# A block product with seven terms for the first values of the second mixer, its weight sums loaded from HBM

## The chip, the cores and the metric

The kernel runs on one core of one Trainium2 chip. The metric is the device time of one execution in microseconds; lower is better. The kernel before takes 923.96 us, the median of three runs (923.92 to 923.99). Line numbers (L354) are those of the kernel before.

## The reference, cut to what matters

A trunk of two layers works on 256 tokens of width 1024. Each layer adds half of a SwiGLU network of width 2816, then a mixer, then half of a second such network. The mixer of the second layer, in which the change lies, is block-sparse attention; at 256 tokens there is one block, so it is causal softmax attention with 16 heads of 64:

```python
def c_mixer(x, w_in, w_out):
    q, k, v = jnp.split(x @ w_in, 3, axis=-1)          # x: (256, 1024), w_in: (1024, 3072)
    o = moba_attention(to_heads(q, 16, 64), to_heads(k, 16, 64), to_heads(v, 16, 64))
    return from_heads(o) @ w_out

for layer in range(2):
    h = h + 0.5 * swiglu(rms_norm(h, ffn1_norm[layer]), ...)
    h = h + mixer(rms_norm(h, mix_norm[layer]))         # layer 0: ab_mixer, layer 1: c_mixer
    h = h + 0.5 * swiglu(rms_norm(h, ffn2_norm[layer]), ...)
```

All is float32. What the change touches is `v = x @ w_in[:, 2048:2560]`, the values of the first eight heads: a product of 256x1024 by 1024x512.

## The kernel before, in words

**Numbers in two parts.** Every float32 operand of a matrix product is split into a high part (rounded to the matmul's format) and a low remainder. A product of two such operands is three matmuls: high by high, high by low, low by high (`mm3`, L353 to L356). ScalarE (ACT) writes the high part of a weight chunk (`whi`, L231), VectorE (DVE) the remainder (`wlo`, L238).

**The weight stream.** The host lays all weights out as chunks of up to 1 MB in the order of use (`weight_chunks`). `Stream` loads them on the SyncE queue into three raw buffers (`load_one`, L183), splits them into four pairs of high and low buffers (`SPL = 4`), and hands them to TensorE with `take()`; `free()` gives a pair back. So the split of a chunk can start when TensorE has finished the chunk four places before it, and a raw load when the split three places before it is done. `hold()` stops splits; `release(tc, behind, one)` lets one or all go, placed on ACT and DVE behind the instructions `behind`. `issue_after` orders instructions on one engine only. Within such bounds the order of each engine's instructions is made when the program is built, by a planner with its own estimates of durations; each engine then runs its list in order.

**Six stages** (phases 0 to 5): network, first mixer, network, network, second mixer (phase 4), network. In a network, 22 steps n (one per 1 MB chunk of gate or up weights) are followed by four column blocks c of the down projection, three chunks each. `Next.pair` (L396) adds a finished column block to the residual `x` and forms `xTh` and `xTl`, the scaled input of the next stage, 128 features by 256 tokens each.

**Sums that are made ahead.** The last network (phase 5) already forms most of its down projection by a block product with seven terms (Winograd's form of Strassen's scheme). The sums of weight blocks for it are made during phases 2 and 3: `begin_sums` loads a chunk (`blocks`, L631), makes sums on DVE (L635 to L641) and stores them in HBM (L647), from where the stream loads them later. `AHEAD` lists the steps at which this happens: (phase, n) with n = 4, 8, 12, 16 in phases 2 and 3, and (3, 19).

**The second mixer** (`c_mixer`, L1249) takes its chunks in this order: q0, k0 (queries and keys of heads 0 to 3), two value chunks of 512 features by 512 columns, q1, k1, q2, k2, two more value chunks, q3, k3, output projection. `first_tiles` (L1117) computes q0 and k0 and, between them, the norm of the input (`sums`, a power on GpSimd called `rstd`, `spread`). `token_block` (L1152) computes the values: for each of two chunks, each of two groups of 128 tokens and each of four feature tiles, three matmuls with 128 tokens stationary and 512 weight columns moving, into one PSUM bank for each token group. `put_v` then scales them into `vth` and `vtl` (L1169, L1170). There are eight PSUM banks. `scores`, `turn` (transposes, L1059) and `weighted` of the heads are hung between the tiles by `Slots`: `step()` counts, and the list says what is done at which count. In `put_k` GpSimd (POOL) copies and subtracts parts of the keys (L1000, L1002); in `scores` it scales the probabilities (L1050).

Of the kernel before, what the change touches and what calls it, by code (L numbers as in the profile page):

```python
# [10 lines left out]
F32 = mybir.dt.float32  # L11
# [40 lines left out]
def weight_chunks():  # L52
# [5 lines left out]

    def cols(m, c0, w, cuts=(), reset=0):
        n = CH // w  # L60
        for k in range(0, KD, n):
            add(m, k * 128, n, c0, c0 + w, SHIFT if w == 256 else 0, cuts, reset)

# [64 lines left out]
class Stream:  # L128
# [12 lines left out]
    def add(self, nk, w, shift, cuts, reset, summed, kind):  # L141

        cuts = (*(cuts or (() if reset else (nk / 2,))), nk)
        j = self.chunks
        self.chunks += 1
        for step in (1, 2) if kind != "N" else (0,):
            if step < 2 or kind == "X":
# [15 lines left out]
    def load_one(self, between=lambda i: None, first=False):  # L163
        u = self.loaded
        j, nk, w, loads, step = self.loads[u]
        i = (u - self.wide) % (RAW + SPARE) - RAW if self.wide is not None and u >= self.wide else -1
        raw = self.raw_pool.tile([128, CH], F32, name="raw") if i < 0 else self.spare[i]
        n = nk * w // loads
        for m in range(loads):
            between(m)  # L170
            cs = slice(m * n, (m + 1) * n)
            src = self.weights[j, m * 128 * n : (m + 1) * 128 * n].rearrange("(p c) -> p c", p=128)
            pieces = [(cs, self.sums[j][0] if step else src)]
            if step == 2:
# [25 lines left out]
    def split_parts(self):  # L200
# [20 lines left out]
        def split(a, r):  # L221
# [15 lines left out]
            else:  # L237
                self.made[u] = done, nc.vector.tensor_sub(lo, r, hi.bitcast(F32))  # L238

        if step:  # L240
            q = w // 2
# [70 lines left out]
def trunk(ctx: ExitStack, tc: tile.TileContext, a, out):  # L312
# [61 lines left out]
    class Next:  # L374
# [21 lines left out]
        def pair(self, i, p, row=None, pool=None, squares=True):  # L396
# [14 lines left out]
            return high, self.low  # L411

        def squares(self, i):

# [66 lines left out]

    nxt = None

# [139 lines left out]
    def begin_sums(fp, n):  # L623
# [27 lines left out]
        return sums  # L651

    def ffn(phase):
        nonlocal nxt
        with tc.tile_pool(name="fp", bufs=1) as fp:
            hT = [fp.tile([128, FT, S], F32R, name=n) for n in ("hTh", "hTl")]
# [22 lines left out]

            ready, ahead = [], []  # L680

# [23 lines left out]
            for n in range(FT):  # L705
# [13 lines left out]
                if (phase, n) in AHEAD:  # L719
                    ahead.append(begin_sums(fp, AHEAD.index((phase, n))))  # L720
                if (phase, n - 1) in AHEAD:
                    ahead.append(ahead.pop()())
                if (phase, n - 2) in AHEAD:
                    ahead.pop()()
                if n == late - 1:
# [17 lines left out]
            if last:  # L743
# [4 lines left out]
                return  # L748
            row = norm["half"]
            nxt = Next(phase + 1)  # L750
            for c in range(4):
                b = bank()
                for k0, n in DOWN:
# [7 lines left out]
                    if k0 + n == FT:  # L761
                        nxt.pair(c, b, row, fp)
                    st.free()

# [179 lines left out]

    def make_attention(mp, mask_cols, nheads, v, mix, rows=False):

# [107 lines left out]
        def turn(h):  # L1054
# [5 lines left out]
            if j == 0:  # L1060
                pts[p] = [mp.tile([128, 2, 384], F32R, name=n, bufs=2) for n in ("pth", "ptl")]
            return split(pts[p][0][:, j, :], pts[p][1][:, j, :], tp[:, :384])
# [53 lines left out]

    def first_tiles(put_q, put_k, step, places=None):  # L1117

# [8 lines left out]
        if not places:  # L1127
            st.free()
        w = st.take()
        tile_of(ps4[3], w, 1, range(4))  # L1130
# [5 lines left out]
        else:  # L1136
            nxt.sums()
        tile_of(ps4[2], w, 0)
        step()
        tile_of(ps4[3], w, 1, range(4, KD))  # L1140
# [5 lines left out]
        for j in range(2):  # L1146
            put_q(j, ps4[j])
            put_k(j, ps4[2 + j])
# [3 lines left out]
    def token_block(evict, step):  # L1152
# [9 lines left out]
        for t in range(NT):  # L1162
            evict(t, pb[t])

    def put_v(v, t, p, c0=0):
# [4 lines left out]
        nc.vector.scalar_tensor_tensor(v[1][:, t, cs], p, y, v[0][:, t, cs].bitcast(F32),  # L1170
                                       op0=ALU.mult, op1=ALU.subtract)

# [76 lines left out]
    def c_mixer(phase):  # L1249
        with tc.tile_pool(name="mp", bufs=1) as mp:  # L1250
            mix = mix_tiles(mp)
            v = v_tiles(mp, D)
            put_q, put_k, scores, turn, weighted, put_ks = make_attention(mp, slice(384, 768), 16, v, mix, True)
# [15 lines left out]
            for c in range(4):  # L1269
                if c:  # L1270
                    tiles(put_q, c, step)
                    tiles(put_k, c, step)
                else:
                    first_tiles(put_q, put_k, step)
                if c % 2 == 0:
                    token_block(lambda t, p: put_v(v, t, p, c * 256), step)
            project(mix, MIX2, phase, step)
            assert not slots.events


# [25 lines left out]
def _layout(a):  # L1306
# [6 lines left out]
    for j, (ms, layer, r, n, c0, c1, *how) in enumerate(chunks):  # L1313
# [3 lines left out]
        w = tiles(w)  # L1317
        if how[-1] != "N":
            w = w.reshape(128, 4, -1)[:, [3, 1, 0, 2]]
# [37 lines left out]
```

## Time and profile before

| what | value |
|---|---|
| median of 3 runs | 923.96 us |
| the profiled execution, its own time | 924.17 us |
| its span, first to last instruction | 922.4 us |
| granted TensorE clock | 0.999 |
| busy share of the span: TensorE matmuls, DVE, ACT, POOL | 99%, 75%, 57%, 9% |
| bytes moved by DMA | 202.15 MB, mean 219 GB/s |
| second mixer, value chunks on TensorE | 646.03 to 657.79 us |

The profiled execution lies 0.21 us over the median. A matmul's duration in the trace is modelled and overlaps its neighbours; what a matmul costs is the distance from its start to the start of the next. SyncE's and POOL's DMA queues share 16 DMA engines; a window's "DMA" is their mean busy share.

### The profile page before, as it was taken

To read this page: it belongs to the slowest core of one execution; us is meant where nothing else is said; L and a number is where in the kernel's file an instruction comes from. 1 tells how busy PE (TensorE), PEld (TensorE's weight loads), DVE (VectorE), ACT (ScalarE), POOL (GpSimd) and SP (SyncE) were. 2 spreads that over 40 slices of the span, in tenths; PEclk is the share of its full clock that TensorE was granted. 3 is DMA by queue.
4 is the path that set the end of the run, shared out by engine and by line. 5 is a ranking of instruction groups with operands and counts; after the bars stand their busy time and mean duration, and the time that the engine had idled before them with its cause. 6 is when DMAs were issued, how large, how long until landed. Compare 5 with 4: busy or idle time off the path is not lost.

```text
span 922.4 us, 18258 instructions
## 1 busy us (share of the span) xinstructions
PE 915.0 (99%) x7583; PEld 896.5 (97%) x7583; DVE 689.8 (75%) x1058; ACT 528.4 (57%) x808; POOL 80.8 (9%) x117
## 2 busy tenths in 40 slices
PE   9999999999999999999999999999999999999997
PEld 9999999999999999999999999999999999999886
DVE  7976556587888867655677666667778799978897
ACT  7754444468667545444564444455776777555574
POOL 0000000033310000000000000001565100000002
PEclk9999999999999999999999999999999999999999
DMA  9765554665256677766556878865533466855681
GB/s 325 272 228 183 180 195 174 228 226 181 93 183 230 220 281 266 296 238 218 187 209 236 305 272 313 318 216 192 184 137 137 119 230 225 277 191 206 223 310 60
DMA packets 33985, 202.15 MB, mean 219 GB/s; under 512 B 3904, under 2 KB 6208, under 8 KB 12528
## 3 DMA queue, kind: packets, MB, share of 16 engines
q1 hardware_dynamic: 32400, 197.79, 59.8%
q0 software_dynamic: 496, 1.77, 0.9%
q10 hardware_dynamic: 1008, 1.44, 0.5%
q8 instruction: 59, 0.97, 0.4%
q14 instruction: 22, 0.18, 0.1%
HBM read 188.14 MB, written 12.85 MB: 218 GB/s over the span
## 4 chain that ended last, share of the span: by engine, by line
PE 93%; issue 4%; DMA 2%; POOL 0%; DVE 0%; ACT 0%; POOLq 0%; DVEq 0%
PE bank L354 30%; PE bank L355 30%; PE bank L356 30%; DMA raw<-in_weights 1%; PE bank L1059 1%; DMA x<-blocks 1%; PE bank L601 1%; DMA xTl<-away 0%; POOL xTl L803 0%; DVE wlo L238 0%; PE bank L604 0%; PE bank L1021 0%; PE bank L1023 0%; PE bank L1022 0%; PE bank L1208 0%
## 5 line engine op out<-in xcount | busy, mean ns | idle before, releaser
L231 ACT ACTIVATE whi<-raw 128x1024 fp32r<-128x1024 f32 (+5 forms) x349 | 331.6, 994 | 280.4 <-issue 154.6
L238 DVE TENSOR_TENSOR wlo<-raw,whi 128x1024 fp32r<-128x1024 f32 (+5 forms) x349 | 390.6, 1149 | 78.8 <-ACT whi L231 77.8
L354 PE MATMUL bank<-xTh,whi 128*128 128x256 f32 x1600 | 442.7, 277 | 0.0
L356 PE MATMUL bank<-xTh,wlo 128*128 128x256 f32 x1600 | 441.8, 276 | 0.0
L355 PE MATMUL bank<-xTl,whi 128*128 128x256 f32 x1600 | 441.8, 276 | 0.0
L355 PEld LDWEIGHTS bank<-xTl,whi 128*128 128x128 f32 x1600 | 300.4, 188 | 0.0
L354 PEld LDWEIGHTS bank<-xTh,whi 128*128 128x128 f32 x1600 | 300.4, 188 | 0.0
L356 PEld LDWEIGHTS bank<-xTh,wlo 128*128 128x128 f32 x1600 | 300.4, 188 | 0.0
L356 PE MATMUL bank<-hTh,wlo 128*128 128x256 f32 x528 | 145.7, 276 | 0.0
L354 PE MATMUL bank<-hTh,whi 128*128 128x256 f32 x528 | 145.7, 276 | 0.0
L355 PE MATMUL bank<-hTl,whi 128*128 128x256 f32 x528 | 145.7, 276 | 0.0
L355 PEld LDWEIGHTS bank<-hTl,whi 128*128 128x128 f32 x528 | 99.1, 188 | 0.0
L354 PEld LDWEIGHTS bank<-hTh,whi 128*128 128x128 f32 x528 | 99.1, 188 | 0.0
L356 PEld LDWEIGHTS bank<-hTh,wlo 128*128 128x128 f32 x528 | 99.1, 188 | 0.0
L687 DVE TENSOR_TENSOR hm<-gs,bank 128x512 f32<-128x512 f32 x44 | 29.9, 683 | 45.4 <-PE bank L356 44.4
L954 POOL MEMSET k<- 64x256 f32 x12 | 3.2, 307 | 565.2 <-ACT whi L231 378.9
L684 DVE TENSOR_TENSOR gs<-bank,row 128x512 f32<-128x512 f32 x44 | 30.1, 686 | 21.3 <-PE bank L356 21.1
L354 PE MATMUL bank<-mixh,whi 128*128 128x256 f32 x128 | 35.7, 279 | 0.0
L356 PE MATMUL bank<-mixh,wlo 128*128 128x256 f32 x128 | 35.4, 277 | 0.0
L355 PE MATMUL bank<-mixl,whi 128*128 128x256 f32 x128 | 35.4, 276 | 0.0
L1050 POOL TENSOR_SCALAR pr<-pr,rl 128x128 f32<-128x128 f32 (+1 forms) x36 | 31.9, 899 | 29.5 <-DVE rl L1046 20.5
L359 ACT ACTIVATE hTh<-hm 128x512 fp32r<-128x512 f32 x44 | 27.1, 619 | 8.8 <-DVE hm L687 8.0
(231 smaller groups left out, 994.1 us busy)
## 6 DMA issues: line engine op xcount, KB each, us to landing
raw<-in_weights SPq DMA_DIRECT2D x139, 1024.0 KB, 5.0
raw<-in_weights SPq DMA_DIRECT2D x12, 768.0 KB, 4.8
blocks<-in_weights SPq DMA_DIRECT2D x9, 1024.0 KB, 10.0
blocks<-blocks SPq DMA_DIRECT2D x9, 1024.0 KB, 8.7
raw<-blocks SPq DMA_DIRECT2D x7, 1024.0 KB, 4.8
raw<-in_weights SPq DMA_DIRECT2D x6, 512.0 KB, 6.6
raw<-in_weights SPq DMA_DIRECT2D x7, 256.0 KB, 5.7
blocks<-block SPq DMA_DIRECT2D x5, 256.0 KB, 8.9
```

Of the source, the lines that this page charges most:

```text
L231: done = nc.scalar.activation(hi, r, AF.Copy)
L238: self.made[u] = done, nc.vector.tensor_sub(lo, r, hi.bitcast(F32))
L354: nc.tensor.matmul(p, sh, mh, start=start, stop=False)
L355: nc.tensor.matmul(p, sh, ml, start=False, stop=False)
L356: return nc.tensor.matmul(p, sl, mh, start=False, stop=stop)
L359: return nc.scalar.activation(hi, src, AF.Copy), nc.vector.tensor_sub(lo, src, hi.bitcast(F32))
L601: nc.tensor.matmul(o, w[0][i][:, cs], xT[m][:, k], start=k == 0 and m == "h" and j % 2 == 0, stop=False)
L684: nc.vector.tensor_mul(g, both(pg), twice(norm["row"]))
L687: nc.vector.tensor_mul(hm, g, both(pu))
L954: nc.gpsimd.memset(pair[j][o, 1].bitcast(F32), 0.0)
L1050: share = engine.tensor_scalar(pr[:, cs], pr[:, cs], rl[:, b : b + 1], None, op0=ALU.mult)
L1059: nc.tensor.transpose(tp[:, i * 128 : (i + 1) * 128], pr[:, i * 128 : (i + 1) * 128], ident)
```

## The change

The first 512 value columns (not the second) are computed by seven block products instead of eight. For each pair of feature tiles (256 features), 256 tokens and 512 columns, the operands are cut into 2x2 blocks: x into 128 features by 128 tokens, w into 128 features by 256 columns. Seven products of blocks or of sums of blocks are collected over the four feature pairs in seven half banks (four banks), and are combined at the end.

- **Weight sums.** During phase 2, at n = 5 and n = 12, `begin_formed` loads one of the two value chunks, makes four sums of blocks for each of its two feature pairs on DVE, splits them into high and low parts, and stores these in HBM: four stores of 512 KB a chunk.
- **Stream.** A value chunk of the new kind "V" becomes two units, one for a feature pair: a raw load of 384 KB with three plain blocks (split as before) and two DMAs from the POOL queue, 512 KB each, that bring the stored high and low parts of the four sums straight into the unit's `whi` and `wlo` buffers.
- **Input sums.** During the down projection of phase 3, `Next.form` makes four sums of blocks of the scaled input after each of the column blocks 0 to 2 and splits them; the fourth is made inside `first_tiles`, into a part of the mixer's own output tiles that is still unused.
- **Products.** `token_sevens` takes the place of `token_block`: 4 units x 7 products x 3 matmuls of 256 moving columns. Afterwards five DVE additions fold the products into `cv`, and `put_v` reads that. Three steps of the slots lie behind the first three units, the fourth behind the fold.
- **Order.** `put_q` of the first two head pairs is moved ahead of k0. Splits are held from the third value unit on: q2's is let go behind `turn(1)`, k2's behind `turn(3)`, all others behind `scores(5)`. The turned probabilities get a pool of their own, and in phases 2 and 3 the blocks of `begin_sums` too.

The core of the diff:

```diff
+FORMED = {(2, 5): 0, (2, 12): 1}
...
-            cols(wc, 2048 + c * 256, 512)
+            cols(wc, 2048 + c * 256, 512, kind="N" if c else "V")
...
+            if step > 2:
+                pieces = [(slice(0, 768), src[:, (step - 3) * 1024 : (step - 3) * 1024 + 768])]
...
+        if step > 2:
+            self.parts[u] = tuple([t[:, shift + i * 256 : shift + (i + 1) * 256] for i in range(7)] for t in (his, los))
+            for to, v in zip((his, los), self.sums[j][step - 3]):
+                nc.gpsimd.dma_start(to[:, shift + 768 : shift + 1792], v)
+            split(shift, raw[:, :768])
...
+        def form(self, i, f, hi, lo):
+            a11, a21, a12, a22 = (x1(2 * i + k)[:, t * 128 : (t + 1) * 128] for k in range(2) for t in range(NT))
+            g0, g1 = (self.gain(2 * i + k) for k in range(2))
+            m, s1, s2, s4 = (f[:, j] for j in range(4))
+            nc.vector.tensor_scalar(m, a22, g1, None, op0=ALU.mult)
+            for to, a, g, b, op in ((s1, a21, g0, m, ALU.add), (s2, a11, g0, s1, ALU.subtract),
+                                    (s4, a12, g1, s2, ALU.add)):
+                nc.vector.scalar_tensor_tensor(to, a, g, b, op0=ALU.mult, op1=op)
+            nc.vector.tensor_add(m, m, s2)
+            split(hi, lo, f)
...
+    def begin_formed(gp, i):
+        j = [n for n, c in enumerate(weight_chunks()) if c[-1] == "V"][i]
+        t = gp.tile([128, CH], F32, name="blocks", bufs=2)
+        with tc.issue_after(st.last.ins):
+            nc.sync.dma_start(t, st.weights[j].rearrange("(p c) -> p c", p=128))
+        yield
+        b = t.rearrange("p (k i c) -> p k i c", k=2, i=4)
+        b11, b21, b22, b12 = (b[:, :, i] for i in range(4))
+        nc.vector.tensor_sub(b11, b12, b11)
+        nc.vector.tensor_sub(b12, b22, b12)
+        nc.vector.tensor_sub(b22, b11, b22)
+        nc.vector.tensor_add(b21, b21, b22)
+        st.sums[j] = [[dram.tile([128, 1024], F32, name=f"formed{i}{k}{m}") for m in "hl"] for k in range(2)]
+        for k in range(2):
+            f = t[:, k * 1024 : (k + 1) * 1024]
+            hi = gp.tile([128, 1024], F32R, name="formed")
+            lo = f.bitcast(F32R)
+            split(hi, lo, f)
+            yield
+            with tc.issue_after(st.last.ins):
+                for to, v in zip(st.sums[j][k], (hi, lo)):
+                    nc.sync.dma_start(to, v.bitcast(F32))
+            yield
...
+    def token_sevens(mix, v, p1, step):
+        own = [m[:, a : a + 2].rearrange("p k t c -> p (k t) c") for m, a in zip(mix, (6, 2))]
+        pb = [bank() for _ in range(4)]
+        at = {1: (0, 0), 2: (0, 1), 6: (1, 0), 5: (2, 0), 7: (2, 1), 3: (3, 0), 4: (3, 1)}
+        p = {n: pb[b][:, h * S : (h + 1) * S] for n, (b, h) in at.items()}
+        for i in range(KD // 2):
+            w = st.take()
...
+            for n, x, q in ((1, plain(0, 0), 0), (2, plain(0, 1), 1), (6, formed(2), 5), (5, formed(1), 3),
+                            (7, formed(0), 6), (3, formed(3), 2), (4, plain(1, 1), 4)):
+                mm3(p[n], *x, w[0][q], w[1][q], i == 0 and at[n][1] == 0, i == KD // 2 - 1 and n in (2, 6, 7, 4))
+                if i == 3 and n == 2:
+                    nc.scalar.activation(p1, p[1], AF.Copy)
+            if i < 3:
+                step()
+            if i == 2:
+                st.hold()
+            st.free()
...
+            nc.vector.tensor_add(u[:, 0], p1, p[6])
+            nc.vector.tensor_add(cv[:, 0], p1, p[2])
+            nc.vector.tensor_add(u[:, 1:], both(pb[2]), twice(u[:, 0]))
+            nc.vector.tensor_add(cv[:, 1:3], u[:, 1:], both(pb[3]))
+            nc.vector.tensor_add(cv[:, 3], u[:, 2], p[5])
+            for t in range(NT):
+                put_v(v, t, cv[:, 2 * t : 2 * t + 2].rearrange("p h c -> p (h c)"))
+            step()
...
-            slots.at((5, 6, 7, 8, 12, 13, 14, 16, 17, 18, 19, 20, 24, 24, 25), scores)
+            slots.at((5, 6, 7, 8, 12), scores)
+            slots.at((13,), lambda _: st.release(tc, scores(5)))
+            slots.at((14, 16, 17, 18, 19, 20, 24, 24, 25), lambda i: scores(6 + i))
...
-            slots.at((9, 9, 11, 11, 16, 16, 19, 19, 21, 21, 23), turn)
+            slots.at((9,), lambda _: turn(0))
+            slots.at((9,), lambda _: st.release(tc, turn(1), True))
+            slots.at((11,), lambda _: turn(2))
+            slots.at((11,), lambda _: st.release(tc, turn(3), True))
+            slots.at((16, 16, 19, 19, 21, 21, 23), lambda i: turn(4 + i))
```

More of the change, by code (lines that the diff above doesn't have):

```diff
@@ L145, in add @@
         self.chunks += 1
-        for step in (1, 2) if kind != "N" else (0,):
-            if step < 2 or kind == "X":
+        for step in {"N": (0,), "V": (3, 4)}.get(kind, (1, 2)):
+            if step != 2 or kind == "X":
                 if step == 1 and self.wide is None:
@@ L238, in split @@
                 self.made[u] = done, nc.vector.tensor_sub(lo, r, hi.bitcast(F32))
+        if step > 2:
[4 more added lines that the diff above has]
+            yield
+            self.read += 1
+            self.split += 1
+            return
         if step:
@@ L678, in turn_back @@
                     nc.sync.dma_start(away[t], xn)
-            ready, ahead = [], []
+            ready, ahead, forming = [], [], []
             def gated(k, pg, pu):
@@ L719, in ffn @@
                 if (phase, n) in AHEAD:
-                    ahead.append(begin_sums(fp, AHEAD.index((phase, n))))
+                    ahead.append(begin_sums(gp, AHEAD.index((phase, n))))
                 if (phase, n - 1) in AHEAD:
@@ L724, in ffn @@
                     ahead.pop()()
+                if (phase, n) in FORMED:
+                    forming.append(begin_formed(gp, FORMED[phase, n]))
+                for g in forming:
+                    next(g, None)
                 if n == late - 1:
@@ L749, in ffn @@
             row = norm["half"]
+            for g in forming:
+                assert next(g, None) is None
+            early_stage.close()
             nxt = Next(phase + 1)
+            if phase == 3:
+                forms = tc.tile_pool(name="sp", bufs=1, side="right")
+                sp = forms.__enter__()
+                nxt.forms = [sp.tile([128, KD // 2 - 1, 4, 128], F32R, name=m) for m in ("sxh", "sxl")]
+                f = fp.tile([128, 4, 128], F32, name="sums")
             for c in range(4):
@@ L762, in ffn @@
                         nxt.pair(c, b, row, fp)
+                        if phase == 3 and c < 3:
+                            nxt.form(c, f, *(s[:, c] for s in nxt.forms))
                     st.free()
@@ L1060, in turn @@
             if j == 0:
[L1061 removed]
+                pts[p] = [(turned or [mp])[0].tile([128, 2, 384], F32R, name=n, bufs=2) for n in ("pth", "ptl")]
             return split(pts[p][0][:, j, :], pts[p][1][:, j, :], tp[:, :384])
@@ L1115, in tiles, with first_tiles @@
         st.free()
-    def first_tiles(put_q, put_k, step, places=None):
+    def first_tiles(put_q, put_k, step, places=None, then=None):
         if places:
@@ L1128, in first_tiles @@
             st.free()
+            for j in range(2):
+                put_q(j, ps4[j])
         w = st.take()
@@ L1138, in first_tiles @@
         tile_of(ps4[2], w, 0)
+        if then:
+            then()
         step()
@@ L1146, in first_tiles @@
         for j in range(2):
-            put_q(j, ps4[j])
+            if places:
+                put_q(j, ps4[j])
             put_k(j, ps4[2 + j])
@@ L1163, in token_block, with plain, formed @@
             evict(t, pb[t])
+    def token_sevens(mix, v, p1, step):
[5 more added lines that the diff above has]
+            w = st.take()
+            def plain(t, k):
+                return [xT[m][:, 2 * i + k, t * 128 : (t + 1) * 128] for m in "hl"]
+            def formed(j):
+                return [s[:, j] if i == 3 else s[:, i, j] for s in (own if i == 3 else nxt.forms)]
+            for n, x, q in ((1, plain(0, 0), 0), (2, plain(0, 1), 1), (6, formed(2), 5), (5, formed(1), 3),
[8 more added lines that the diff above has]
+            st.free()
+        forms.__exit__(None, None, None)
+        with tc.tile_pool(name="fold", bufs=1, side="right") as fold:
+            u = fold.tile([128, 3, S], F32, name="u")
+            cv = fold.tile([128, 4, S], F32, name="cv")
+            nc.vector.tensor_add(u[:, 0], p1, p[6])
[6 more added lines that the diff above has]
+            step()
     def put_v(v, t, p, c0=0):
@@ L1273, in c_mixer, with formed @@
                 else:
-                    first_tiles(put_q, put_k, step)
-                if c % 2 == 0:
+                    own = [m[:, a : a + 2].rearrange("p k t c -> p (k t) c") for m, a in zip(mix, (6, 2))]
+                    p1 = mp.tile([128, S], F32, name="first")
+                    def formed():
+                        f = wk.tile([128, 2, S], F32, name="sq", bufs=1)
+                        nxt.form(3, f.rearrange("p t (j c) -> p (t j) c", j=2), *own)
+                    first_tiles(put_q, put_k, step, then=formed)
+                    token_sevens(mix, v, p1, step)
+                    late = tc.tile_pool(name="late", bufs=1, side="right")
+                    turned.append(late.__enter__())
+                if c == 2:
                     token_block(lambda t, p: put_v(v, t, p, c * 256), step)
@@ L1278, in c_mixer @@
             assert not slots.events
+            late.__exit__(None, None, None)
     ffn(0)
```

29 lines of the change are left out of this document (17 added, 12 removed).

## The prediction

> **What bounds the kernel now.** I read the page first: who is busy, and the chain that ended last.
>
> ```profile
> span 922.4 us, 18258 instructions
> PE 915.0 (99%) x7583; PEld 896.5 (97%) x7583; DVE 689.8 (75%) x1058; ACT 528.4 (57%) x808; POOL 80.8 (9%) x117
> PE   9999999999999999999999999999999999999997
> ...
> PE 93%; issue 4%; DMA 2%; POOL 0%; DVE 0%; ACT 0%; POOLq 0%; DVEq 0%
> ```
>
> TensorE is busy in every slice but the last and carries 93% of the chain. A busy PE can still hide stalls, as durations overlap, so I read start distances in its timeline: first a stretch of a network, then the value chunks.
>
> ```profile
> 534.76 0.28 PE L354 MATMUL bank<-xTh,whi 128*128 128x256 f32 x1
> ...
> 556.98 0.28 PE L355 MATMUL bank<-xTl,whi 128*128 128x256 f32 x1
> ...
> 645.66 0.28 PE L356 MATMUL bank<-xTh,wlo 128*128 128x256 f32 x1
> ...
> 646.03 0.48 PE L354 MATMUL bank<-whi,xTh 128*128 128x512 f32 x1
> ...
> 646.82 0.39 PE L354 MATMUL bank<-whi,xTh 128*128 128x512 f32 x1
> ...
> 651.36 0.39 PE L356 MATMUL bank<-whi,xTl 128*128 128x512 f32 x1
> 651.59 0.28 PE L1021 MATMUL bank<-k,q 128*128 128x256 f32 x1
> ...
> 651.94 0.40 PE L354 MATMUL bank<-whi,xTh 128*128 128x512 f32 x1
> ...
> 654.69 0.28 PE L1021 MATMUL bank<-k,q 128*128 128x256 f32 x1
> ...
> 655.04 0.40 PE L354 MATMUL bank<-whi,xTh 128*128 128x512 f32 x1
> ...
> 657.79 0.63 PE L1030 MATMUL bank<-k,q 128*128 128x256 f32 x4
> ```
>
> The first two rows are 196 starts apart: 22.22 / 196 = 0.1134 us for 256 moving columns. From 646.82 to 651.36 there are 20 starts: 0.227 us for 512 columns, twice the other. So TensorE is limited by columns, nothing else, and the second mixer has no stall to win back: between the rows lie matmuls, and only the two changes of operand cost a few hundredths more. Only columns taken away can shorten this kernel; new waits can lengthen it.
>
> **The change part by part.**
>
> *Matmuls.* Away go 2 chunks x 2 token groups x 4 features x 3 = 48 of 512 columns. In the trace they take 657.79 - 646.03 = 11.76 less two groups of scores (651.59 to 651.94, 654.69 to 655.04: 0.70), 11.06 us; by the clean distance 48 x 0.227 = 10.90. In come 4 units x 7 products x 3 = 84 of 256 columns: 84 x 0.1134 = 9.52 us. The gain is 1.38 (clean) to 1.54 (as traced). I take 1.45, between them, since the new stretch has the same interleaved scores and will lose part of those hundredths too.
>
> *DVE and ACT work.*
>
> ```profile
> L238 DVE TENSOR_TENSOR wlo<-raw,whi 128x1024 fp32r<-128x1024 f32 x279 | 334.4, 1227 | 46.9 <-ACT whi L231 46.1
> L359 DVE TENSOR_TENSOR hTl<-hm,hTh 128x512 fp32r<-128x512 f32 x44 | 30.1, 685 | 1.4 <-ACT hTh L359 1.4
> L238 DVE TENSOR_TENSOR wlo<-raw,whi 128x768 fp32r<-128x768 f32 x25 | 22.8, 952 | 23.7 <-ACT whi L231 23.5
> L635 DVE TENSOR_TENSOR blocks<-blocks 128x512 f32<-128x512 f32 x9 | 6.2, 693 | 25.4 <-DMA blocks<-in_weights 25.4
> L426 DVE TENSOR_TENSOR acc<-acc,sq 128x256 f32<-128x256 f32 x12 | 5.0, 417 | 0.3 <-ACT sq L416 0.2
> L694 DVE SCALAR_TENSOR_TENSOR gs<-hm 128x128 f32<-128x128 f32 x9 | 2.6, 288 | 0.2
> L697 DVE TENSOR_SCALAR hm<-hm 128x128 f32<-128x128 f32 x9 | 2.0, 219 | 0.0
> ```
>
> ```profile
> 314.00:336.00 22.00, 22.00 (x197) 22.00 (x196) 14.85 (x18) 10.30 (x13) 0.00 (x0) 1.00 0.88 309
> 336.00:358.00 22.00, 22.00 (x197) 22.00 (x196) 14.87 (x17) 10.47 (x14) 0.00 (x0) 1.00 0.75 267
> 358.00:380.00 22.00, 22.00 (x197) 22.00 (x196) 16.14 (x19) 10.60 (x13) 0.00 (x0) 1.00 0.76 285
> 380.00:402.00 22.00, 22.00 (x196) 22.00 (x196) 14.15 (x17) 10.16 (x13) 0.00 (x0) 1.00 0.70 265
> 630.00:646.00 16.00, 16.00 (x143) 16.00 (x142) 11.96 (x19) 9.75 (x17) 3.63 (x10) 1.00 0.59 208
> 646.00:658.00 12.00, 12.00 (x59) 10.06 (x58) 8.67 (x18) 9.77 (x20) 8.17 (x10) 1.00 0.53 184
> ```
>
> (Columns: window, length, busy PE, PE loads, DVE, ACT, POOL, clock, DMA share, GB/s.) Phase 2, `begin_formed`: a chunk costs DVE 4 x 0.69 + 2 x 1.23 = 5.2 us, 10.4 for both, where DVE has 6 to 8 us free in every 22: hidden, zero on the path. One `form`: 0.22 + 3 x 0.29 + 0.28 + 0.69 = 2.1 us on DVE, three of them in 60 us of down projection: hidden by the four-chunk lead of the splits. The fourth falls into 630 to 646 with 4 us free, where the split of two chunks (4 x 1.23) becomes four shorter ones (4 x 0.95) with three of them in that window: hidden. The fold: 3 x 0.42 + 2 x 0.69 = 2.6 us on DVE behind the last product, ahead of `put_v`; the values are first used by `weighted(0)` at count 11, four tiles of queries and keys (4 x 24 x 0.1134 = 10.9 us) later, so 4 us of fold and scaling are covered. It also frees four banks instead of two: the first next matmuls take two others, and the moved `put_q` frees two early. Without that cover the price would be the fold, 2.6. Holding the splits of q2, k2 and later keeps them behind the fold and softmax work; each is let go one tile pair (48 x 0.1134 = 5.4 us) ahead of its use against 2.5 us of DVE and 2.1 of ACT: 0 here, at most some tenths behind `scores(5)`.
>
> *DMA in phase 2.* Each chunk is 1.05 MB read and 2.10 written. At 309 / 0.88 = 351 GB/s both cost the DMA engines 6.29 / 0.351 = 18 us. The four windows are busy 68 of 88 us; 18 more just fit, with a backlog of some 6 us early. Splits start four chunks (4 x 5.4 us) ahead of TensorE and raw loads three ahead of that, so 6 us reach nobody: 0; with 16 us of backlog the first matmul would wait.
>
> *The reload, the one thing on the path.* Each unit needs 2 x 512 KB through POOL into buffers that TensorE frees four units earlier. For the fourth unit that is the end of k0: 645.66 + 0.11 = 645.8. It is needed at its third product: 646.03 + 63 x 0.1134 + 0.70 of scores + 6 x 0.1134 = 654.55. The nearest rows are the two other POOL DMAs of 512 KB:
>
> ```profile
> L236 POOL DMA_DIRECT2D wlo<-in_weights x2: 852/898/943, 719.7 to 721.5; - x2
> DMA to landing us min/median/max: 5.9/7.8/9.6
> ```
>
> ```profile
> 721.60:724.00 2.40, 2.40 (x22) 2.31 (x20) 1.60 (x8) 1.38 (x7) 0.79 (x1) 1.00 0.87 150
> ```
>
> ```profile
> raw<-in_weights SPq DMA_DIRECT2D x139, 1024.0 KB, 5.0
> ```
>
> POOL is occupied 0.9 us by each issue, so the second one starts at 646.7 and lands at 652.6 (5.9) to 656.3 (9.6): 2.0 us early to 1.7 late. The trace's pair adds to what stands in the buffer, and in 721.6 to 724, where it is alone, moves only 150 / 0.87 = 172 GB/s; a plain load moves 208 / 0.59 = 353 and lands 1 MB in 5.0. The new ones only write, so I take the near end: 0 stall, bounds 0 and 1.7. The fit that the Trainium skill gives for such DMAs ("DMA: Bandwidth & Descriptors", section "Anatomy of one DMA — SWDGE (gpsimd) path"), 2.0 us plus the bytes at 436 GB/s, would be an estimate of 3.2 us and leave 4.6 us of room; the two rows above are longer, and no run yet shows a plain one of this size.
>
> **Sum.** -1.45 + 0 = -1.45 us on the profiled execution's 924.17, 922.7; on the median, 0.21 lower, 922.5, a ratio of 0.9984.
>
> **The rivals.**
>
> *A: the last unit comes a little late, the gain is eaten.* The 1.7 us above, and POOL next to DVE:
>
> ```profile
> 649.27 1.13 POOL L1000 CAST k<-k 64x256 fp32r<-64x256 f32 x1 [6.12 <-ACT k L998]
> 651.27 0.39 POOL L1000 CAST k<-k 64x256 fp32r<-64x256 f32 x1
> ...
> 655.12 1.62 POOL L1002 TENSOR_TENSOR k<-qk,k 64x256 fp32r<-64x256 f32 x1
> ```
>
> ```profile
> 648.93 1.21 DVE L238 TENSOR_TENSOR wlo<-raw,whi 128x1024 fp32r<-128x1024 f32 x1
> ```
>
> The same cast takes 0.39 us alone and 1.13 while DVE subtracts a split. If each of the two issues is held as long (0.74), the second lands 1.5 us later, the stall is 0 to 3.2 us: 922.5 to 925.7, still within 0.2%. The Trainium skill states this as a rule ("SBUF — State Buffer", section "SBUF: two separate sides"): GpSimd shares a port pair with DVE under a lock and cannot write the descriptors of its DMAs meanwhile. By that rule the trace agrees, as far as a cast can show it.
>
> *B: slower, the eight reloads move at the rate of the adding pair.* They convert float32 into the matmul's format, as that pair does, and could share its 172 GB/s. Then 4.19 MB take 24.4 us, the raw loads of v3, q1 and k1 beside them (2.5 MB at 0.353) 7.1. The first can start when the last but one down chunk is done, 645.8 less 132 matmuls and 0.6 of small ones, 630.2, with data from about 632, after two issues of 0.9; the last ends at 663.5, 9 us late: 931.5. It decides below some 224 GB/s: 632 to 654.55, plus the 3.3 us of stall that make the kernel 0.2% slower, less 7.1, leave 18.7 us for 4.19 MB. For it: same queue, same formats. Against: the slow rate goes with reading the destination.
>
> *C: slower, wrong order on POOL.* In the program the key copies stand ahead of the fourth unit's DMAs; behind them (1.62 from 655.12) the second issue is at 657.6, lands at 663.5: also 931.5. Against it, the same choice on ACT:
>
> ```profile
> 645.91 1.06 ACT L231 ACTIVATE whi<-raw 128x1024 fp32r<-128x1024 f32 x1 [1.64 <-issue]
> 647.00 0.39 ACT L478 ACTIVATE row<-bank 128x256 f32<-128x256 f32 x1
> ```
>
> The split that waits for the same buffer was put ahead of the norm's work, as it was ready first.
>
> *D: faster by over 0.2%* needs 1.85 us, more than the 1.54 of the traced columns; nothing else on the path is touched.
>
> **How the numbers follow.** A measurement of this kernel tells about 0.2% (1.85 us) from no change. The forecast has 0.58; A 0.16; B 0.14; C and a backlog in phase 2 that reaches TensorE 0.07; D 0.05. So faster 0.05, same 0.58 + 0.16 = 0.74, slower 0.21. The forecast alone spans 922.0 to 923.0 (the gain's two ends and some tenths). The range goes from 922.0 over all of A (925.7) into the mild part of B, 926.5; D and most of B and C, some 0.19, are left out.
>
> **What would show it.** Right: 84 matmuls of 256 columns in the value stretch at 0.113 us, first to last about 10.3 us with the scores, and no start distance over 0.3 us there. Wrong by A or B: a gap on TensorE ahead of the third product of the fourth (or third) unit, with POOL DMAs landing over 8.8 us after k0's end, and their rate in a window where they run alone. Wrong by C: the DMAs behind the casts in POOL's timeline. DVE too full: a gap ahead of the tiles of q1 or k1, or ahead of `turn(0)`. Phase 2: start distances over 0.12 us between 300 and 400.

## The result, and the profile after

The changed kernel takes 929.57 us (median of 6 runs, 929.24 to 929.88) where the kernel before took 923.98 beside it (6 runs, 923.69 to 924.18): a ratio of 1.0061, 95% interval 1.0048 to 1.0073. The forecast was 922.5. The profiled execution has a span of 927.6 us against 922.4. Line numbers of the changed kernel are higher by 3 (`whi` L234, `wlo` L241), 12 (`mm3` L366 to L368) and 64 (the mixer).

The page first: busy engines, TensorE by slices, the chain that ended last.

```profile
span 927.6 us, 18435 instructions
PE 915.5 (99%) x7619; PEld 897.0 (97%) x7619; DVE 708.5 (76%) x1099; ACT 534.3 (58%) x817; POOL 88.2 (10%) x125
PE   9999999999999999999999999999989999999997
...
DMA  9765554665256899955557878749453466855681
...
PE 87%; issue 5%; DVE 3%; ACT 2%; DMA 2%; POOL 1%; SPq 0%; POOLq 0%; DVEq 0%; ACTq 0%
```

TensorE now has a slice below 9 ahead of the last, from 673 to 696 us, and its share of the chain fell from 93% to 87% in favour of DVE, ACT and POOL. So something on those engines holds it, late in the second mixer, not in the value stretch that the change rewrote. That stretch in TensorE's timeline:

```profile
645.53 0.36 PE L366 MATMUL bank<-whi,xTh 128*128 128x256 f32 x1
...
656.13 0.63 PE L1094 MATMUL bank<-k,q 128*128 128x256 f32 x4
```

From 645.53 to 656.13 are 10.60 us where 11.76 stood before: a gain of 1.16, 0.29 short of the forecast, as the start distance is 0.117 to 0.118 in most of it. Then TensorE's waits from 640 to 705 us, by what ended them. In the kernel before, this view is empty.

```profile
PE bank L1085 <- POOL k L1066: 1.6, 1, 1.6
PE bank L1123 <- DVE nm L1104: 1.2, 1, 1.2
PE bank L366 <- DVE mixl L1139: 0.8, 1, 0.8
PE bank L367 <- DVE wlo L241: 0.5, 1, 0.5
PE bank L367 <- DVE ptl L371: 0.4, 1, 0.4
```

(Total, times, longest.) That is 4.5 us of waits, all from the second value block (c = 2) to the transposes behind it. Measured by start distances, from the first matmul of that block to the first of q3, the stretch took 14.78 us before and 20.54 now, 5.76 more (first the kernel before, then the changed one):

```profile
684.88 0.40 PE L354 MATMUL bank<-whi,xTh 128*128 128x512 f32 x1
...
699.66 0.36 PE L354 MATMUL bank<-xTh,whi 128*128 128x256 f32 x1
```

```profile
683.82 0.40 PE L366 MATMUL bank<-whi,xTh 128*128 128x512 f32 x1
...
704.36 0.36 PE L366 MATMUL bank<-xTh,whi 128*128 128x256 f32 x1
```

What is late there is seen in the splits on ACT and DVE: first the kernel before, the last chunk of the second value block, and then the changed kernel, where all four splits of the block come in a row.

```profile
672.12 1.07 ACT L231 ACTIVATE whi<-raw 128x1024 fp32r<-128x1024 f32 x1
673.22 1.33 DVE L238 TENSOR_TENSOR wlo<-raw,whi 128x1024 fp32r<-128x1024 f32 x1 [1.69 <-ACT whi L231]
675.50 1.07 ACT L231 ACTIVATE whi<-raw 128x1024 fp32r<-128x1024 f32 x1
676.60 1.35 DVE L238 TENSOR_TENSOR wlo<-raw,whi 128x1024 fp32r<-128x1024 f32 x1 [0.23 <-ACT whi L231]
```

```profile
682.22 0.19 ACT L1107 ACTIVATION_READ_ACCUMULATOR pr<-pr,nm 128x1 f32 x1
682.31 3.90 ACT L234 ACTIVATE whi<-raw 128x1024 fp32r<-128x1024 f32 x4
683.39 4.83 DVE L241 TENSOR_TENSOR wlo<-raw,whi 128x1024 fp32r<-128x1024 f32 x4 [0.72 <-ACT whi L234]
684.67 0.50 PE L367 MATMUL bank<-wlo,xTh 128*128 128x512 f32 x1 [0.46 <-DVE wlo L241]
```

The first row is the end of the exponential of `scores(5)`, the instruction behind which the last release puts everything. Splits that were done at 678 now end at 688.2, while TensorE asks for the first at 683.8; then the split of q3, the scaling of k2's keys and POOL's key copies are late behind them.

The books, in offsets of the two timelines: the start 0.50 us earlier (initial loads), the value stretch -1.16, the next 27 us +0.60 (the same slower start distance), the second value block +5.76; from 705 us on every matmul has the same offset, 4.70, to the last one; +0.58 behind the last matmul (0.30 in the order of the last norm's work on DVE and ACT, 0.28 from the last stores to the end of the span). Together 5.3, the difference of the spans.

### The profile page after: what moved, and what is told of

Same layout as the page of the kernel before. It is cut to its first block, busy times and chain, and to the rows that moved or that the text cites. A ratio compares the mean times of both kernels' runs of the same rounds, so it can differ in the third digit from the quotient of the medians.

```text
span 927.6 us, 18435 instructions
## 1 busy us (share of the span) xinstructions
PE 915.5 (99%) x7619; PEld 897.0 (97%) x7619; DVE 708.5 (76%) x1099; ACT 534.3 (58%) x817; POOL 88.2 (10%) x125
## 4 chain that ended last, share of the span: by engine, by line
PE 87%; issue 5%; DVE 3%; ACT 2%; DMA 2%; POOL 1%; SPq 0%; POOLq 0%; DVEq 0%; ACTq 0%
PE bank L367 28%; PE bank L366 28%; PE bank L368 28%; DVE wlo L241 2%; PE bank L625 1%; DMA x<-blocks 1%; ACT whi L234 1%; PE bank L1123 1%; ACT pr L1107 0%; DMA xTl<-away 0%; DMA raw<-in_weights 0%; POOL xTl L867 0%; PE bank L628 0%; ACT k L1062 0%; DVE pr L1104 0%
## 5 line engine op out<-in xcount | busy, mean ns | idle before, releaser
L234 ACT ACTIVATE whi<-raw 128x1024 fp32r<-128x1024 f32 (+5 forms) x349 | 330.9, 991 | 271.4 <-issue 138.7
L241 DVE TENSOR_TENSOR wlo<-raw,whi 128x1024 fp32r<-128x1024 f32 (+5 forms) x349 | 389.7, 1147 | 72.8 <-ACT whi L234 71.5
L366 PE MATMUL bank<-xTh,whi 128*128 128x256 f32 x1600 | 442.9, 277 | 0.0
L368 PE MATMUL bank<-xTh,wlo 128*128 128x256 f32 x1600 | 442.0, 276 | 0.0
L366 PEld LDWEIGHTS bank<-xTh,whi 128*128 128x128 f32 x1600 | 300.4, 188 | 0.0
L368 PEld LDWEIGHTS bank<-xTh,wlo 128*128 128x128 f32 x1600 | 300.4, 188 | 0.0
L366 PE MATMUL bank<-hTh,whi 128*128 128x256 f32 x528 | 145.7, 276 | 0.0
L368 PE MATMUL bank<-hTh,wlo 128*128 128x256 f32 x528 | 145.7, 276 | 0.0
L368 PEld LDWEIGHTS bank<-hTh,wlo 128*128 128x128 f32 x528 | 99.1, 188 | 0.0
L366 PEld LDWEIGHTS bank<-hTh,whi 128*128 128x128 f32 x528 | 99.1, 188 | 0.0
L1114 POOL TENSOR_SCALAR pr<-pr,rl 128x128 f32<-128x128 f32 (+1 forms) x36 | 35.3, 991 | 27.5 <-DVE rl L1110 25.7
L366 PE MATMUL bank<-mixh,whi 128*128 128x256 f32 x128 | 35.7, 279 | 0.0
L368 PE MATMUL bank<-mixh,wlo 128*128 128x256 f32 x128 | 35.4, 277 | 0.0
```

The costliest lines, as they stand in the source:

```text
L234: done = nc.scalar.activation(hi, r, AF.Copy)
L366: nc.tensor.matmul(p, sh, mh, start=start, stop=False)
L368: return nc.tensor.matmul(p, sl, mh, start=False, stop=stop)
L1114: share = engine.tensor_scalar(pr[:, cs], pr[:, cs], rl[:, b : b + 1], None, op0=ALU.mult)
```

## The experiments

"The products" are the seven block products with all that belongs to them, "the hold" is `st.hold()` with its releases. v2a and v2b are the two chunks of the second value block. Where no number of runs is given, there were 5. Beside these runs the kernel before had medians of 923.71 to 923.94.

**1. The hold alone, in the kernel before.** `token_block` calls `st.hold()` before its first `free()` for c = 0, and the releases are those of the change:

```diff
+            if held and i == 0:
+                st.hold()
...
+            slots.at((13,), lambda _: st.release(tc, scores(5)))
```

> The kernel before, with all four plain value chunks and none of the sums, plus only the hold behind its second value chunk and the same three releases (one split behind turn(1), one behind turn(3), the rest behind scores(5)). T1: the same 5 to 6 us of stalls at the second value block, 923.98 + 5.8 = 929.8, between 928.5 and 931. T2 (the added work on VectorE is at fault): 924 to 925, as nothing is added to VectorE. T3 with late reloads: 924, as there are no reloads.

Measured: 928.61 us, ratio 1.0052 (1.0040 to 1.0065). No product is changed, nothing is added to VectorE, and 4.8 us are lost. Its splits and its waits:

```profile
682.32 3.90 ACT L231 ACTIVATE whi<-raw 128x1024 fp32r<-128x1024 f32 x4
683.40 4.83 DVE L238 TENSOR_TENSOR wlo<-raw,whi 128x1024 fp32r<-128x1024 f32 x4 [0.72 <-ACT whi L231]
```

```profile
PE bank L1021 <- POOL k L1002: 1.6, 1, 1.6
PE bank L1059 <- DVE nm L1040: 1.2, 1, 1.2
PE bank L355 <- DVE ptl L359: 0.4, 1, 0.4
PE bank L354 <- DVE mixl L1075: 0.2, 1, 0.2
```

The same splits at the same times within 0.01 us as in the changed kernel, and three of its five waits to the tenth; the other two are smaller, as TensorE comes later here. T1 holds here, T2 and T3 fall as causes of this loss. It also shows where the 1.16 us went: the last matmul of k2 starts at 685.05 in this kernel and at 683.71 in the changed one, and both go on with q3 at 704.37 and 704.36. In this stretch DVE, ACT and POOL set the time, so a lead of TensorE is waited away.

That the times are so equal from 667 us on is in part luck. This profiled run comes to its value stretch 0.79 us later than the changed kernel's (646.32 against 645.53), and between 655 and 667 DVE idles up to 1.39 us at a time here and never more than 0.25 in the changed kernel, which has more to do there. A measure without the start is the time from the first matmul of the value stretch to the first of q3: 53.63 us before, 58.05 here, 58.83 in the changed kernel. From there to the last matmul it is 216.4 us in all kernels of this document. So on top of the hold the products cost some 0.8 us in this stretch instead of gaining.

**2. The products without the hold.** `st.hold()` and the three releases are taken out of the changed kernel.

> The changed kernel without the hold: the splits of q2, k2 and the chunks behind them are issued as soon as their buffers come free, as in the kernel before; the seven products, the formed sums, the reload and the fold stay. Theory T1 (the last, full release behind the softmax of scores(5) makes the splits for the second value block some 10 us late, and 5.76 us of stalls between 683 and 704 come from nothing else): those stalls go, 929.57 - 5.8 = 923.8 us, between 923.0 and 924.5, so at or just below the kernel before (923.98), and the value stretch stays at 10.6 us. Theory T2 (the added work on VectorE, fold and forming, is what makes the second mixer late, whoever holds the splits): it stays above 928. Theory T3 (raw loads or reloads land late): it stays above 928 too, with DMA as the releaser of the splits at 688 to 691.

Measured: 930.22 us, ratio 1.0068 (1.0055 to 1.0080). My T1 expected 923.8: a clear miss. The time is "above 928", as T2 and T3 had it; of T3's late DMAs one shows, for 0.4 us. The late stalls are gone (no wait from 680 to 705), others have come:

```profile
PE bank L1123 <- POOL pr L1114: 2.6, 2, 2.4
PE bank L1123 <- DVE cv L1262: 0.8, 1, 0.8
PE bank L366 <- DVE cv L1264: 0.7, 1, 0.7
PE bank L367 <- DMA wlo<-formed11l: 0.4, 1, 0.4
```

`cv` is the fold, `pr` the softmax. In DVE's timeline the first addition of the fold starts at 662.64; between 655.66 and 664.2 stand six splits of 1.2 us. In the changed kernel the fold starts at 657.78. So the hold does serve a purpose: the four value units take 2.6 us each and each gives a buffer pair back, so that four splits of whole chunks fall due in 10.6 us, where the two value chunks of before gave back two in 11.8. Without a hold they go ahead of the fold and the softmax, with it they are late for the second value block. Theory T1b: a heap of splits on either side hurts.

**3. Other places for the last release.** Three variants of the changed kernel: everything that is still held is let go behind `turn(1)` (count 9), behind `turn(3)` (count 11), or behind `scores(6)` (count 14); the one-split releases ahead of that stay.

```diff
-            slots.at((9,), lambda _: st.release(tc, turn(1), True))
+            slots.at((9,), lambda _: st.release(tc, turn(1)))
```

> The changed kernel with everything let go at once behind turn(1) at count 9: q2, k2 and v2a as one heap of six splits of 1.2 us in VectorE's queue ahead of the scaling of k1. T1b: the heap is ahead of qk and of the keys of k1, which PE needs at 674, so a wait of 2 to 3 us there in place of the 5.8 at 684 to 704, and the later splits are in time: 926 to 928. T1 in its first form (only late splits cost, so the sooner the better): 924 to 925.

> The changed kernel with the hold, its one-split release behind turn(1) as it is, but everything let go behind turn(3) at count 11 instead of behind scores(5) at count 13. T1: the splits of the second value block start at about 674 instead of 682.3, close to the 672 to 675 of the kernel before, so 923 to 925. T2 and T3: 928 or more. T4 (any hold costs, since the raw buffers come free later and the loads behind them too): about half the loss stays, 926 to 927.

> The changed kernel with the last release one step later, behind scores(6) at count 14 instead of scores(5) at 13. T1: a tile pair's half later (24 matmuls of 256 columns, 2.8 us), the same chain of splits, so the stalls grow by 1.5 to 3 us: 931 to 932.6. T2 and T3: nothing depends on the place of the release, 929 to 930.

Measured: 929.21 (ratio 1.0058, 1.0045 to 1.0072), 929.73 (1.0065, 1.0052 to 1.0078) and 929.12 us (1.0054, 1.0040 to 1.0068). The time hardly depends on the place, though the waits do: one line each from the waits of the kernels released at 9, 11 and 14.

```profile
PE bank L1085 <- POOL k L1066: 3.7, 1, 3.7
```

```profile
PE bank L1123 <- POOL pr L1114: 2.9, 3, 1.9
```

```profile
PE bank L366 <- ACT whi L234: 2.3, 1, 2.3
```

Released at 9, the heap stands ahead of the scaling of k1's keys; at 11 it stands ahead of the softmax of `scores(4)` (DVE subtracts for 5.63 us in a row from 674.49); at 14, v2a itself is 2.3 us late. T1 in its first form, the sooner the better, fails on all three, and T4 on the second. At 14 the 929 to 930 of T2 and T3 came out, though experiment 1 rules out their causes for the loss of the hold. T1b expected 926 to 928 for the first and was still too low, for a reason that the windows of that kernel show (length, PE, loads, DVE, ACT, POOL, clock, DMA, GB/s):

```profile
674.00:678.00 4.00, 0.38 (x3) 0.39 (x4) 3.96 (x8) 3.03 (x6) 1.49 (x3) 1.00 0.99 354
678.00:682.00 4.00, 4.00 (x25) 4.00 (x25) 3.86 (x9) 1.39 (x3) 3.74 (x5) 0.63 0.63 227
```

Behind the wait the granted clock falls to 0.63 in the window. It is 0.50 from 679.0 to 682.4, where 16 matmuls in a row take 0.213 us each instead of 0.118: 1.5 us lost on top of the 3.9. The other two show it as well (512 columns at 0.427 us instead of 0.227; some 2.2 us lost at count 11, where it lasts 6.8 us, and 1.7 at count 14). The waits of the changed kernel, at most 1.98 us from start to start, cost no clock.

**4. The held splits spread out.** q2 and k2 one by one behind `turn(1)`, v2a behind `turn(3)`, v2b behind `scores(4)`, the rest behind `scores(5)`:

```diff
-            slots.at((9,), lambda _: st.release(tc, turn(1), True))
+            def twice1(_):
+                behind = turn(1)
+                st.release(tc, behind, True)
+                st.release(tc, behind, True)
+            slots.at((9,), twice1)
...
-            slots.at((5, 6, 7, 8, 12), scores)
+            slots.at((5, 6, 7, 8), scores)
+            slots.at((12,), lambda _: st.release(tc, scores(4), True))
```

> The changed kernel with each held split let go one step sooner: q2 and k2 behind turn(1), the first half of the second value block (v2a) behind turn(3), the other (v2b) behind scores(4), the rest behind scores(5). The runs so far: without any hold 930.22 (VectorE gives seven splits in a row before the fold and the softmax, PE waits at 654 to 677), all let go at turn(3) 929.73 (a heap of six splits ahead of the softmax of scores(4), PE waits at 687 to 692 for turns), at scores(5) 929.57 and scores(6) 929.12 (v2a and v2b late). Theory T1b (either side of the softmax of scores(4) and scores(5) a heap of splits hurts; spread out they fit, since VectorE is idle 1 to 2 us at 669 to 673): stalls between 645 and 705 fall below 1 us, 923.3 to 924.5. Theory T2b (VectorE has too much to do in this stretch, whatever the order, because of fold, forming and put_v at full width): 927 or more.

Measured: 925.90 us (10 runs), ratio 1.0024 (1.0014 to 1.0033), 3.7 us better than the changed kernel. T2b (927 or more whatever the order) falls; T1b's 923.3 to 924.5 is missed by 1.4 us. Two variants with less of the spreading, k2 and v2a together behind `turn(3)`, and v2a alone behind `scores(4)` with the rest as in the change:

> The changed kernel with q2 let go behind turn(1) as it is, k2 and v2a together behind turn(3), v2b behind scores(4), the rest behind scores(5). T1b: four splits of 1.2 us on VectorE ahead of the softmax of scores(4), which moves it by 2.4 us to 681, about where scores(5) has it in the kernel before: 923.5 to 925.5, little or no stall at 688 and 692. T2b: 927 or more.

> The changed kernel with v2a alone let go behind scores(4), and v2b and the rest behind scores(5). T1b: the splits of v2a start at about 680 instead of 682.3, still after the softmax of scores(4), so the stall at 683.8 shrinks by some 2 us and the ones behind it less: 926 to 928.5. T2b: as the changed kernel, 929 to 930.

Measured: 928.61 (ratio 1.0058, 1.0044 to 1.0071) and 927.09 us (1.0036, 1.0023 to 1.0048). The first is a miss for T1b (and lies where T2b had it): four splits in a row ahead of the softmax of `scores(4)` were too many, PE waits 2.9 us for the probabilities at 687 to 691 and then runs at the lower clock, 0.57 from 691 to 694. The second is as expected.

**5. Is what is left the hold or the products?** The spread releases of 4 in the kernel before, without the products.

> The kernel before, without the seven products, with the hold and the sooner releases of e5 (q2 and k2 behind turn(1), v2a behind turn(3), v2b behind scores(4), the rest behind scores(5)). It is the missing cell beside e4 (hold and late releases without the products, 928.61), the changed kernel (both, 929.57), e5 (products with sooner releases, 925.90), e1 (products without a hold, 930.22) and the kernel before (neither, 923.8). Theory H (what is left in e5 is the hold, which puts the splits of v2b and q3 some 2.4 us later than in the kernel before): 925.3 to 926.2, with the wait ahead of the turns at 700. Theory F (what is left in e5 is the products' own work on VectorE, fold and forming): 923.8 to 924.6.

Measured: 925.61 us (11 runs), ratio 1.0020 (1.0011 to 1.0028): theory H. The waits of this kernel and, below, of experiment 4:

```profile
PE bank L1059 <- POOL pr L1050: 0.8, 2, 0.6
PE bank L355 <- DVE ptl L359: 0.2, 1, 0.2
```

```profile
PE bank L1123 <- POOL pr L1114: 0.8, 2, 0.6
PE bank L1085 <- POOL k L1066: 0.2, 1, 0.2
```

The same 0.8 us ahead of the turns at 700. From the value stretch to q3 it is 55.35 us here and 55.32 in experiment 4, so with these releases the products neither gain nor lose there. The 0.29 us between the medians fits what lies behind the last matmul: from its start to the end of the span it is 6.32 us in the three profiled kernels without the products and 6.60 to 6.91 in the eleven with them. Why is open. The six cells, medians in us:

| | no hold | hold, late releases | hold, spread releases |
|---|---|---|---|
| without the products | 923.8 | 928.61 | 925.61 |
| with the products | 930.22 | 929.57 | 925.90 |

**6. The fold.** In the second kernel of experiment 7 the values are taken straight from two banks, and the five additions are left out.

> The kernel of e9 with the fold left out: the values are taken straight from two of the four banks, so the block sums of the values are not formed (2.6 us of VectorE gone, the values differ); matmuls, splits, hold and releases stay. Theory T2b (behind the spread of the splits what is left of the loss, some 2 us of waits at 674, 695 and 700, is the fold's 2.6 us in VectorE's queue, which push the split of v2b and q3 behind them by as much): 923.0 to 924.0, 1.5 to 2.2 us below e9. Theory T1b alone (only the places of the releases matter): within 0.5 us of e9.

Measured: 925.45 us (11 runs), ratio 1.0017 (1.0009 to 1.0026), 0.7 below that kernel, with intervals that overlap. That is between the two theories, and nearer T1b. The profiled run has lost the wait at 674 (POOL's key copies, 0.7 us in experiment 7), but not the one ahead of the turns, and it shows a wait for a reload instead (this one execution took 926.53 us, 1.1 over the median):

```profile
PE bank L367 <- DMA wlo<-formed11l: 1.0, 1, 1.0
PE bank L1123 <- POOL pr L1114: 0.8, 2, 0.6
```

So once the release is mended the fold reaches the path, by 0.7 us or so, not by 2.6; how much exactly these runs don't tell.

**7. The start distance.** The value units at the start of their buffers, alone and together with the spread releases:

```diff
-            add(..., SHIFT if w == 256 or kind == "V" else 0, ...)
+            add(..., SHIFT if w == 256 else 0, ...)
```

> The changed kernel with the value units written at the start of the split buffers instead of 16 elements behind it; all else as it is. In the changed kernel the start distance of 256 moving columns is 0.1175 us from 645.7 to 648.8 and again from 651.9 to 680, where the kernel before settles at 0.1134 some nine matmuls after each interruption. Theory P1 (the place of the moving operand in its buffer sets the pace): the distance in the value stretch changes, to 0.1134 or to over 0.118, 929.0 or 930 us. Theory P2 (a pace that the stream falls into at an interruption and keeps, whatever the address): the stretch stays at 0.117 and the time at 929.5.

> The two edits that helped, together: held splits one step sooner (q2 and k2 behind turn(1), v2a behind turn(3), v2b behind scores(4), the rest behind scores(5)), and the value units at the start of their buffers. With the splits sooner alone the time was 925.9. Theory P1 (the place in the buffer sets the pace behind the value stretch): the 120 matmuls of q1 to q2 run at 0.1134 instead of 0.1178, 0.5 us, and part of the value stretch too; nothing is swallowed by a stall now, so 925.0 to 925.5. Theory P2 (the pace is chance): 925.9.

Measured: 929.65 (ratio 1.0065, 1.0052 to 1.0077) and 926.15 us (8 runs, 1.0027, 1.0016 to 1.0038). The text ahead of the second counts both edits as helping; the times of the first, 929.65 against 929.57, don't show that. Behind the value stretch the distance does fall to 0.1134, as P1 says for that part: first the first and last matmul of the tile at 660 to 663 in the unshifted kernel, then the same two in the changed one.

```profile
660.43 0.28 PE L366 MATMUL bank<-xTh,whi 128*128 128x256 f32 x1
...
663.04 0.28 PE L368 MATMUL bank<-xTh,wlo 128*128 128x256 f32 x1
```

```profile
659.77 0.28 PE L366 MATMUL bank<-xTh,whi 128*128 128x256 f32 x1
...
662.48 0.28 PE L368 MATMUL bank<-xTh,wlo 128*128 128x256 f32 x1
```

Over the 23 starts between them these are 0.1135 and 0.1178. In the value stretch itself the distance rises, from 0.1178 to 0.120 us in most of it, which P1 allowed for too. No time is gained: alone, the waits behind it grow by as much; with the spread releases, PE asks for k1's keys at 673.5 instead of 673.9 and gets them at 674.48 instead of 674.44. P1 is right on the pace in that part and wrong on its price. Why a stream that uses other buffers is slowed by the place of the units before it stays open.

## Why the prediction failed

**The step that failed** is one sentence of the part on DVE and ACT: "each is let go one tile pair (48 x 0.1134 = 5.4 us) ahead of its use against 2.5 us of DVE and 2.1 of ACT: 0 here, at most some tenths behind `scores(5)`". It measured 4.8 us, by experiment 1. Three things were wrong in it. The last release lets two chunks go, not one: 3.90 us of ACT and 4.83 of DVE, not 2.1 and 2.5. Its time was counted in tiles of TensorE, but it hangs on the end of a softmax: the trace of before had that exponential of `scores(5)` end on ACT at 684.4 (the row below), hardly ahead of the value block at 684.88, and I didn't read the row. And the question "what is late next" was answered for the held splits alone: behind them stood q3's split, the key scaling and POOL's copies. That the splits of v2b ran at 672 to 678 before, 14 us ahead of their use at 691.7, was in the same view.

```profile
684.25 0.19 ACT L1043 ACTIVATION_READ_ACCUMULATOR pr<-pr,nm 128x1 f32 x1
```

A second term of the sum failed with it, the -1.45 for the matmuls. It took for granted that a gain on TensorE in the value stretch reaches the end. It does not: with the hold and late releases the products cost 0.96 us (929.57 against 928.61), with spread releases 0.29 (925.90 against 925.61), and without the hold 6.4 (930.22 against 923.8); 0.3 to 0.6 of each lies behind the last matmul (experiment 5), where the sum had nothing. So dropping the hold would not have saved the forecast: the splits then stand ahead of the fold and the softmax on DVE.

None of the rivals had this mechanism: none priced the wait that the change adds.

**Right.** The matmuls: 84 of 256 columns in place of 48 of 512. The gain was 1.16 instead of 1.45 where it arises, as the distance was 0.117 to 0.118 instead of 0.1134, and nothing in the end. Phase 2: its DMA share rose to 0.8 and 0.9 (the page's DMA row, slices 14 to 17) and TensorE had no start distance over the usual one there. The fold, the forming of the input sums and the four banks end no wait of TensorE in the changed kernel, as said. The cover of the fold was partly the lateness of others, since it ends waits of 1.5 us in experiment 2 and is worth some 0.7 in experiment 6.

**The reload.** In the profiled changed kernel the last DMA landed in time. The bounds of 5.9 to 9.6 us from issue to landing were fair (5.7 to 9.6 over the eleven kernels), which one run would not have told: first the changed kernel, then the kernels of experiment 3 (count 14) and of experiment 6.

```profile
wlo<-formed11l POOLq DMA_DIRECT2D x1, 512.0 KB, 5.7
```

```profile
wlo<-formed11l POOLq DMA_DIRECT2D x1, 512.0 KB, 8.9
```

```profile
wlo<-formed11l POOLq DMA_DIRECT2D x1, 512.0 KB, 9.6
```

In five of the eleven kernels TensorE starts late for it, with a start distance of 0.3 to 1.3 us (0.8 and 1.3 in the last two). So rival A is real in some kernels, and didn't happen in the profiled changed one. Its second half did not show at all: the issue of the last reload takes POOL 0.54 us from 646.20 on, beside a subtraction of DVE from 646.23, and an issue with DVE idle at 630.95 takes the same; the forecast had 0.9, and 0.74 more if held. B (172 GB/s for all eight, the last landing at 663.5) and C (DMAs behind the casts) are refuted: in the changed kernel the last reload lands at 651.9, and the first cast behind it starts at 648.11. The 3.2 us that the Trainium skill's fit gives ("DMA: Bandwidth & Descriptors", section "Anatomy of one DMA — SWDGE (gpsimd) path") were met by no reload; the shortest was 4.5.

**The best that was found** is 925.90 us for the products with spread releases. It beats the changed kernel and not the kernel before. VectorE has little room where the splits fall due (DVE is the third number with a count in each row; before, then the changed kernel):

```profile
655.00:660.00 5.00, 5.00 (x34) 4.51 (x32) 4.17 (x14) 3.15 (x9) 4.49 (x6) 1.00 0.54 195
660.00:665.00 5.00, 5.00 (x47) 5.00 (x46) 4.57 (x10) 2.59 (x7) 2.45 (x3) 1.00 0.29 93
665.00:670.00 5.00, 5.00 (x47) 5.00 (x46) 3.59 (x9) 4.35 (x10) 1.50 (x2) 1.00 0.35 144
```

```profile
655.00:660.00 5.00, 5.00 (x44) 5.00 (x44) 5.00 (x15) 1.95 (x8) 2.36 (x3) 1.00 0.79 261
660.00:665.00 5.00, 5.00 (x45) 5.00 (x44) 4.62 (x15) 4.36 (x12) 2.73 (x4) 1.00 0.39 164
665.00:670.00 5.00, 5.00 (x43) 4.94 (x42) 4.89 (x11) 3.13 (x7) 1.75 (x3) 1.00 0.00 0
```

DVE is busy 14.5 of 15 us here, 12.3 before. A share of 76% over the span said nothing of it. There is room on both sides in the changed kernel (DVE is busy 3.70 of 5 us from 650 to 655 and 2.52 from 670 to 675), so that another order could still win is not excluded.

## What to carry to other kernels

Price a wait that a change adds from the trace's own rows: when the releasing instruction ended, how much work it lets go at once, and what stands behind that work on the same engine. An engine at 75% of the span can be full in the one stage where work is added, so take its busy time in windows of 5 us there. Before a matmul is shortened, ask what sets the next point at which TensorE meets the other engines: if they set it, the time saved is waited away.

## What the hardware showed that I had not expected

- **A wait on TensorE can cost twice.** In five kernels the granted clock falls to 0.50 behind waits, for 3.4 us in four of them and 6.8 in the one released at count 11; 256 columns then take 0.213 us and 512 take 0.427. The waits ahead of it were single ones of 2.3, 2.4 and 3.7 us (experiments 3, 2 and 3), one of 0.57 and one of 1.91 close together (experiment 3, count 11), and three of 0.55, 0.75 and 1.57 close together (experiment 4). Behind waits of up to 1.6 us, further apart, the clock stayed at 1.00. The Trainium skill has this as a clock gate that looks at activity in windows of some 3.4 us which run freely ("TensorE: Matmul & The Clock Gate", section "Part 1: The HAM clock gate"); the runs agree with half speed, and waits shorter than such a window were enough.
- **Three paces of the same matmul.** At a granted clock of 1.00, 256 columns go at 0.1134 us, at 0.1178 or, in the value stretch of experiment 7, at 0.120. A stream changes pace mostly at an interruption by other operands, and it can keep the slower one across several of them (0.1178 from 653.3 to 676.9 us in the changed kernel). Moving the operands of one stage by 16 elements in their buffers changed the pace of that stage and of the next. The cause is open.
- **POOL's copies beside DVE.** In the chain of key copies a cast takes 0.39 us, and 1.28 at 674.38 in the changed kernel, while DVE subtracts a split: so a heap of splits delays keys twice, in DVE's queue and on POOL.
